# Ten of thirty convolution taps moved from VectorE to ScalarE and accumulating transfers

## The chip, the core and the metric

The kernel runs on one core of one Trainium2 chip. The metric is the device time of one execution in microseconds (us). Before the change the median of three runs is 1334.81 us.

The engines are called by the profile's names. PE is the matrix engine (TensorE), PEld its weight loads, DVE is VectorE, ACT is ScalarE, POOL is GpSimd and SP is SyncE. POOL and SP issue transfers (DMAs). Each engine works through its own instructions in a fixed order; an instruction whose inputs are not there holds up everything behind it on that engine.

## What is computed

One decoder layer over 1024 tokens of width 1024, in float32. Eleven 1024-wide projections of the normalised input feed three branches: a gated spatial mixing (A), a convolution module (B) and a cross-attention into 256 memory tokens (C). Each branch is projected, gated and summed, and an output projection and a norm follow. The change is in branch B:

```python
glu = z[..., OFF_B_A:OFF_B_A + W] * jax.nn.sigmoid(z[..., OFF_B_B:OFF_B_B + W])
c = causal_depthwise_conv(glu, conv_w[l], conv_b[l])     # 31 taps: position t sees t-30..t
c = jax.nn.silu(layer_norm(c, conv_ln_g[l], conv_ln_b[l]))
```

## The kernel before

**Tiles.** Features lie on the 128 partitions and tokens along the row, so a tile of 128 features by 1024 tokens is 512 KB. There are eight such tiles of the convolution, called conv tile 0 to 7 here. `slot()` hands out 36 buffers of that size (`NSLOT`) for everything that lives long: projection results, operands, branch values.

**Stages, in order of time.** Keys and values of the memory (to about 72 us); the first projection of branch A (to about 149 us); the other ten projections (149 to 928 us); the branch projections with the attention between them (928 to 1249 us); the output projection (to the end).

**The ten projections.** The loop at L546 goes over p = 0 to 3 and, inside, over ten blocks. Each call of `pair` (L373) makes two tiles of one block by seven products instead of eight (Strassen's scheme), each product being 12 matmuls of 128x512. float32 precision comes from splitting every operand into a high and a low part: ACT casts the high part (`split`, L74) and DVE subtracts it from the source to get the low part (L75). There are six operand buffers (`NOP`, tag `op`), so the two engines run a few products ahead of PE. Of a product's result in PSUM, ACT copies pieces (`p1` L383, `u2` L397, `u3` L404) and DVE adds others (L391, L405, L414); then ACT applies the block's function to the two result tiles `ca` and `cb` (L421 to L427), and POOL stores them. The matmuls of product `x<-T` for `os3` (L402) go on accumulating in the bank that the copy `u2` (L397) reads, so they wait for that copy. ACT's L421, the function of the previous pair's `ca`, stands just ahead of L397, and reads what DVE's L414 writes.

**The convolution.** `conv` (L449) is a generator: each of its steps is one DVE instruction. The first sets the accumulator `a` to the newest tap times the input plus the bias (L452), then thirty instructions (L456) each add one more tap, shifted by one token; then `a` is stored and added into `csum`. The generators of two tiles are queued in `todo` after block 1 of each p, and `pump` (L437) takes a few steps after each pair and eight after each branch tile (L727).

**The handover at about 928 us.** Merge 0 (`merge(0, 0)`, L725) projects branch A: 48 matmuls over eight feature tiles `bhi`/`blo` in order (L622). Each `bhi`/`blo` pair comes from `branch_tile` (L586): a cast on ACT, a subtraction on DVE. Behind them on DVE stand the low parts of the first attention queries (`ql`), which the score matmuls (L660) read.

**What sets the order.** A scheduler places all instructions of an engine in one list ahead of time. What the change does to these lists is shown below as rows of the built programs.

Of the kernel before, what the change touches and what calls it, by code (L numbers as in the profile page):

```python
# [10 lines left out]
AF = mybir.ActivationFunctionType  # L11
ALU = mybir.AluOpType
# [6 lines left out]
S = 1024  # L19
# [7 lines left out]
TAPS = 31  # L27
PAD = TAPS - 1
# [6 lines left out]
COL_CW = 56  # L35
# [4 lines left out]
def trunk(ctx, tc, xt, x, memt, wf, wv, wkf, wkv, wbr, wo, wst, bs, cols, fng, out):  # L40
    nc = tc.nc
    V, A, G, T = nc.vector, nc.scalar, nc.gpsimd, nc.tensor

    const = ctx.enter_context(tc.tile_pool(name="const", bufs=1))
    wpool = ctx.enter_context(tc.tile_pool(name="wpool", bufs=2))
    slots = ctx.enter_context(tc.tile_pool(name="slots", bufs=NSLOT))
    small = ctx.enter_context(tc.tile_pool(name="small", bufs=2))
# [10 lines left out]
    def slot(dt=F32, shape=(P, 1024), s="s"):  # L58
        return slots.tile(list(shape), dt, tag="slot", name=nm(s))
# [72 lines left out]
    def store(dst, src):  # L132
        G.dma_start(out=dst, in_=src)
# [6 lines left out]
    def spill(s, dt=F32, shape=(P, S)):  # L140
        return dram.tile(list(shape), dt, name=nm(s))

# [1 line left out]
    ones = const.tile([P, P], F32, name="ones")  # L144
    G.memset(ones, 1.0)
    onesd = const.tile([P, P], F32, name="onesd")
# [3 lines left out]
    col = const.tile([P, NCOL], F32, name="col")  # L150
    A.dma_start(out=col, in_=cols)

    def c1(base, k):
        return col[:, base + k:base + k + 1]

# [1 line left out]
    ahead = []  # L157

    def kv_ahead(n):
# [84 lines left out]
        if e >= XLAG:  # L244
            x_gain(e - XLAG)

# [1 line left out]
    B = [[[None] * 4 for _ in range(2)] for _ in range(2)]  # L248

    def x_norm(k, c):  # L250
# [15 lines left out]
    for hf in range(2):  # L266
        pst = [bank() for _ in range(MT)]
        for c in range(4):
            kv_ahead(KT + hf * 4 + c + NAHEAD)
            hi, lo = wchunk(None, ahead[KT + hf * 4 + c])  # L270
            i = hf * 4 + c
            if i < XLAG:
                x_gain(KT - XLAG + i)
            for m in range(MT):
                ms = slice(m * P, (m + 1) * P)
                for kk2 in range(2):
                    k = 2 * c + kk2
# [25 lines left out]
            split(o, q[:, 0, :], q[:, 1, :])  # L303
            lst.append(q)

# [1 line left out]
    nx = 0  # L307
    vadram = spill("vad", shape=(TT, P, D))
    for th in range(2):
        va = [slot(s="va") for _ in range(4)]  # L310
        for ch in range(2):
            pst = [bank() for _ in range(4)]
            for c in range(4):
                hi, lo = wchunk(None, raw_load(wv[ch * 4 + c], True))
                for t in range(4):
                    ts_ = slice(t * P, (t + 1) * P)
                    for kk2 in range(2):
                        k = 2 * c + kk2
# [5 lines left out]
                i = ch * 4 + c  # L324
# [15 lines left out]
            for t in range(4):  # L340
                A.activation(out=va[t][:, ch * H:(ch + 1) * H], in_=pst[t], func=AF.Gelu_apprx_tanh,
                             scale=1.0 if th else xrs[:, t:t + 1])
# [12 lines left out]
            A.activation(out=va[t], in_=va[t], func=AF.Identity, scale=vr[:, t:t + 1], bias=vm[:, t:t + 1])  # L355
            store(vadram[th * 4 + t], va[t])

# [1 line left out]
    pend = []  # L359

    def prod(ps, w, m, start, stop):
# [70 lines left out]
            then(ca, cb)  # L432
        return go

    todo = []

    def pump(n):  # L437
        while n and todo:
            try:
                next(todo[0])  # L440
                n -= 1
            except StopIteration:
                todo.pop(0)

    cdram = [spill("cd") for _ in range(KT)]

# [2 lines left out]
    def conv(e, g):  # L449
        cw = COL_CW + e * TAPS  # L450
        a = slot(s="conv") if e else csum
        V.tensor_scalar(a, g, col[:, cw + PAD:cw + PAD + 1], c1(COL_CB, e), ALU.mult, ALU.add)  # L452
        yield
        for j in range(PAD):
            n = S - PAD + j
            V.scalar_tensor_tensor(out=a[:, PAD - j:], in0=g[:, :n], scalar=col[:, cw + j:cw + j + 1],  # L456
                                   in1=a[:, PAD - j:], op0=ALU.mult, op1=ALU.add)
            yield
        store(cdram[e], a)
        if e:  # L460
            V.tensor_tensor(csum, csum, a, ALU.add)
            yield
# [16 lines left out]
    def hold(key):  # L479
        def then(ca, cb):  # L480
            held[key] = (ca, cb)
        return then

    def glu(p):
        def then(ca, cb):
            for i, (c, sg) in enumerate(zip((ca, cb), held.pop("b"))):
                V.tensor_tensor(c, c, sg, ALU.mult)
                todo.append(conv(2 * p + i, c))
        return then

    gate = {}
# [27 lines left out]
    def va_load(g):  # L519
        va = slot(shape=(P, TT, P), s="va")  # L520
        nc.sync.dma_start(out=va, in_=vadram[:, :, g * P:(g + 1) * P].rearrange("t p d -> p t d"))
        return va
# [23 lines left out]
    for p in range(4):  # L546
        for i, (blk, fn, then) in enumerate((
            (BLK_BB, sig, hold("b")),
            (BLK_BA, finish, glu(p)),
            (BLK_U, gelu, hold_u(p)),  # L550
            (BLK_GA, silu, ugate(p)),
            (BLK_GC, silu, to_dram(sgcdram)(p)),
            (BLK_GB, silu, to_dram(sgbdram)(p)),
            (BLK_Q, finish, to_dram(qdram)(p)),
            (BLK_M0, sig, to_dram(gdram[0])(p)),
            (BLK_M0 + 2, sig, to_dram(gdram[2])(p)),
            (BLK_M0 + 1, sig, to_dram(gdram[1])(p)),
        )):
            if p == 3 and i == 9:
                for e in range(NPRE):  # L560
                    bra[e] = load(udram[e], s="bra")
            if i == 2:
                spatial_load(p)
            pair(blk, p, kept(fn, then))
            if i == 3:
                for g in range(2 * p, 2 * p + NVA):
                    vas[g] = va_load(g)
            pump(PUMP[i])

# [1 line left out]
    ready = {}  # L571
    order = [(n, d) for n in (0, 2, 1) for d in range(KT)]
    raws = []
# [55 lines left out]
        V.tensor_tensor(g, ps, g, ALU.mult)  # L629
        return g  # L630

    # attention, half of the tokens of a head at a time, in four stages
    unit = {}
    brcdram = spills("brc")

# [121 lines left out]
    for d in range(KT):  # L757
        g = merge(2, d, conv_rstd if d == 4 else None)
# [44 lines left out]
    for d in range(KT):  # L803
        g = load(gdram[1][d], s="gate")
        ps = proj(1, d, bhi, blo)
        w = S if d < KT - 1 else H
        for i in range(0, S, w):
            v = slice(i, i + w)
# [5 lines left out]
        if d == W2AT:  # L814
            w21 = wbase(2)

# [1 line left out]
    def gop(v):  # L818
        o = op()
        split(v, o[:, 0, :], o[:, 1, :])  # L820
# [110 lines left out]
NPRE = 3  # L931
NRDY = 2
NFETCH = 3
NSLOT = 36
NRAW = 3
NOP = 6
NSUM = 4
# [58 lines left out]
```

## Time and profile before

| | before |
|---|---|
| median of three runs | 1334.81 us (1333.74 to 1335.65) |
| span of the profiled execution | 1333.8 us |
| PE busy | 1316.5 us, 99% |
| DVE busy | 1079.5 us, 81% |
| ACT busy | 595.3 us, 45% |
| POOL busy | 61.3 us, 5% |
| transfers, mean over the span | 135 GB/s |

The profile is one execution; its span runs from the first to the last instruction. The median of the timed runs is 1.0 us above that span. A share of busy time is an average over stages with different limits; what a change in one stage is worth is read from that stage's waits. The granted clock of PE is full in all of the 40 slices of the page.

### The profile page before, as it was taken

How to read it: one execution, taken by the hardware profiler on the slowest of the kernel's cores; microseconds unless marked ns; L12 is line 12 of the kernel's file. 1: busy time of each engine (PE TensorE's matmuls, PEld its weight loads, DVE VectorE, ACT ScalarE, POOL GpSimd, SP SyncE). 2: the span in 40 equal slices, each digit the busy share in tenths (PEclk: the TensorE clock that was granted, in tenths of full speed). 3: DMA queues.
4: the chain of work that ended last, by engine and by line, in shares of the span. 5: the costliest groups of instructions: out<-in, count | busy, mean ns of one | idle time of the engine just before them, and what ended most of it. 6: DMA issues, size and time to landing. Idle time of an engine off the chain costs nothing.

```text
span 1333.8 us, 16115 instructions
## 1 busy us (share of the span) xinstructions
PE 1316.5 (99%) x6084; PEld 1098.6 (82%) x6084; DVE 1079.5 (81%) x1438; ACT 595.3 (45%) x967; POOL 61.3 (5%) x120
## 2 busy tenths in 40 slices
PE   8999999999999999999999999999999999999997
PEld 7888888888888888888888888887888888888886
DVE  6799759969966998986996996796797486944797
ACT  6757634334444344434434444345544443502256
POOL 0000000000000000000000000001000010000000
PEclk9999999999999999999999999999999999999999
DMA  9634312342222333223333213338555354633323
GB/s 372 248 110 158 135 62 81 111 142 96 103 78 79 121 118 140 88 79 111 111 110 120 95 48 127 127 111 297 188 181 171 112 190 157 228 119 111 142 96 126
DMA packets 60126, 179.99 MB, mean 135 GB/s; under 512 B 5904, under 2 KB 15248, under 8 KB 60048
## 3 DMA queue, kind: packets, MB, share of 16 engines
q1 hardware_dynamic: 44464, 122.96, 27.2%
q0 software_dynamic: 15296, 55.58, 10.9%
q8 instruction: 47, 0.77, 0.2%
q10 hardware_dynamic: 288, 0.42, 0.1%
q14 instruction: 31, 0.25, 0.1%
HBM read 131.75 MB, written 47.19 MB: 134 GB/s over the span
## 4 chain that ended last, share of the span: by engine, by line
PE 95%; DVE 2%; ACT 1%; issue 0%; DMA 0%; SPq 0%; DVEq 0%; ACTq 0%
PE x L365 33%; PE acc L622 19%; PE y L365 16%; PE z L365 8%; PE b L322 6%; PE acc L841 5%; PE b L231 2%; PE acc L660 2%; PE acc L696 2%; PE b L280 1%; PE sp L534 1%; DMA mraw<-in_memt 0%; DVE xsum L130 0%; PE acc L681 0%; ACT y L874 0%
## 5 line engine op out<-in xcount | busy, mean ns | idle before, releaser
L365 PE MATMUL x<-T,op 128*128 128x512 f32 x1440 | 347.5, 390 | 0.7 <-ACT u L404 0.7
L365 PEld LDWEIGHTS x<-T,op 128*128 128x128 f32 x1440 | 269.8, 188 | 57.4 <-ACT u L404 1.1
L74 ACT CAST op<-sum 128x512 fp32r<-128x512 f32 x160 | 99.5, 622 | 132.2 <-PE z L365 56.4
L456 DVE SCALAR_TENSOR_TENSOR conv<-cb,col,conv 128x994 f32<-128x994 f32 (+14 forms) x120 | 151.8, 1265 | 0.5
L75 DVE TENSOR_TENSOR op<-sum,op 128x512 fp32r<-128x512 f32 x160 | 109.4, 686 | 36.0 <-ACT op L74 35.7
L622 PE MATMUL acc<-bhi,whi 128*128 128x512 f32 x384 | 119.7, 393 | 0.9 <-DVE ca L414 0.9
L622 PE MATMUL acc<-bhi,wlo 128*128 128x512 f32 x384 | 119.1, 390 | 0.0
L622 PE MATMUL acc<-blo,whi 128*128 128x512 f32 x384 | 118.7, 390 | 0.0
L365 PE MATMUL x<-B,op 128*128 128x512 f32 x480 | 115.5, 389 | 0.0
L365 PE MATMUL z<-B,op 128*128 128x512 f32 x480 | 115.3, 389 | 0.0
L365 PE MATMUL y<-T,op 128*128 128x512 f32 x480 | 115.3, 389 | 0.0
L365 PE MATMUL y<-B,op 128*128 128x512 f32 x480 | 115.3, 389 | 0.0
L456 DVE SCALAR_TENSOR_TENSOR conv<-ca,col,conv 128x994 f32<-128x994 f32 (+14 forms) x90 | 113.7, 1263 | 0.2
L74 ACT CAST op<-raw 128x512 fp32r<-128x512 f32 x120 | 74.3, 620 | 79.3 <-PE y L365 77.9
L75 DVE TENSOR_TENSOR op<-raw,op 128x512 fp32r<-128x512 f32 x120 | 82.1, 686 | 33.4 <-ACT op L74 33.4
L365 PEld LDWEIGHTS y<-B,op 128*128 128x128 f32 x480 | 90.1, 188 | 18.7
L365 PEld LDWEIGHTS y<-T,op 128*128 128x128 f32 x480 | 90.1, 188 | 18.7
L365 PEld LDWEIGHTS z<-B,op 128*128 128x128 f32 x480 | 90.1, 188 | 18.7
L365 PEld LDWEIGHTS x<-B,op 128*128 128x128 f32 x480 | 90.1, 188 | 18.7
L622 PEld LDWEIGHTS acc<-blo,whi 128*128 128x128 f32 x384 | 72.1, 188 | 15.5 <-DVE blo L75 0.4
L622 PEld LDWEIGHTS acc<-bhi,wlo 128*128 128x128 f32 x384 | 72.1, 188 | 15.0
L622 PEld LDWEIGHTS acc<-bhi,whi 128*128 128x128 f32 x384 | 71.3, 188 | 15.9 <-issue 1.7
(231 smaller groups left out, 1961.2 us busy)
## 6 DMA issues: line engine op xcount, KB each, us to landing
raw<-in_wf SPq DMA_DIRECT2D x80, 512.0 KB, 3.5
raw<-in_wbr SPq DMA_DIRECT2D x24, 512.0 KB, 4.4
gate<-g SPq DMA_DIRECT2D x24, 512.0 KB, 4.2
raw<-in_wv SPq DMA_DIRECT2D x16, 512.0 KB, 3.6
g<-cb POOLq DMA_DIRECT2D x12, 512.0 KB, 3.1
g<-ca POOLq DMA_DIRECT2D x12, 512.0 KB, 2.9
xr<-in_xt SPq DMA_DIRECT2D x8, 512.0 KB, 10.5
kvraw<-in_wkv SPq DMA_DIRECT2D x8, 512.0 KB, 10.7
```

The source lines that it names most:

```text
L74: A.copy(hi, src)
L75: V.tensor_tensor(lo, src, f(hi), ALU.subtract)
L231: T.matmul(ps[:, :M], w[:, ks], m[k], start=(k == 0 and j == 0), stop=(k == KT - 1 and j == 2))
L280: T.matmul(pst[m], a[k][:, ms], w[:, ws], start=(k == 0 and j == 0), stop=(k == KT - 1 and j == 2))
L322: T.matmul(pst[t], q[:, a, ts_], w[:, ws], start=(k == 0 and j == 0), stop=(k == KT - 1 and j == 2))
L365: T.matmul(ps, w[:, a, ks], m[k][:, b, :], start=(start and k == 0 and j == 0), stop=(stop and k == 3 and j == 2), skip_group_check=not start)
L456: V.scalar_tensor_tensor(out=a[:, PAD - j:], in0=g[:, :n], scalar=col[:, cw + j:cw + j + 1], in1=a[:, PAD - j:], op0=ALU.mult, op1=ALU.add)
L534: T.matmul(ps[:, t * P:(t + 1) * P], va[:, 4 * hf + t, :], ws[:, i, :], start=True, stop=True)
L622: T.matmul(ps[:, hf, :], w[:, ks], m[k][:, hf * H:(hf + 1) * H], start=(k == 0 and j == 0), stop=(k == KT - 1 and j == 2))
L660: T.matmul(ps[:, i, :], q[a][:, d, i * P:(i + 1) * P], kk[:, b, d, :], start=(d == 0 and j == 0), stop=(d == 1 and j == 2))
L696: T.matmul(ps[:, d, :], vv[:, a, m, d * P:(d + 1) * P], p2[b][:, m, :], start=(m == 0 and j == 0), stop=(m == MT - 1 and j == 2))
L841: T.matmul(ps[t], a[k][i][:, ts_], w[k][n], start=(start and k == 0 and j == 0), stop=(k == 3 and j == 2), skip_group_check=not start)
```

## The change

`conv` no longer runs wholly on DVE. ACT sets the accumulator (Identity with scale and bias). For the ten oldest taps ACT writes a scaled copy of the input into a new tile `tap`, and POOL issues a transfer that adds this tile into the accumulator in SBUF, shifted (`accum_op`). The other twenty taps stay on DVE, in a second generator `conv_rest` that is queued when the first is through. The first part has a queue of its own, `early`, of which three steps are taken after each pair, ahead of `pump`; what is left of it is taken after the loop. There are three more slots, and the scratch for transfer descriptors is set to 4096.

```diff
+    todo, early = [], []
+    def run(queue, n):
+        while n and queue:
+            try:
+                next(queue[0])
+                n -= 1
+            except StopIteration:
+                queue.pop(0)
+    def pump(n):
+        run(todo, n)
...
     def conv(e, g):
         cw = COL_CW + e * TAPS
         a = slot(s="conv") if e else csum
-        V.tensor_scalar(a, g, col[:, cw + PAD:cw + PAD + 1], c1(COL_CB, e), ALU.mult, ALU.add)
+        A.activation(out=a, in_=g, func=AF.Identity, scale=col[:, cw + PAD:cw + PAD + 1], bias=c1(COL_CB, e))
         yield
-        for j in range(PAD):
+        for j in range(NACT):
+            n = S - PAD + j
+            t = slot(s="tap")
+            A.activation(out=t[:, :n], in_=g[:, :n], func=AF.Copy, scale=col[:, cw + j:cw + j + 1])
+            G.dma_start(out=a[:, PAD - j:], in_=t[:, :n], accum_op=ALU.add)
+            yield
+        todo.append(conv_rest(e, g, a))
+
+    def conv_rest(e, g, a):
+        cw = COL_CW + e * TAPS
+        for j in range(NACT, PAD):
             n = S - PAD + j
             V.scalar_tensor_tensor(out=a[:, PAD - j:], in0=g[:, :n], scalar=col[:, cw + j:cw + j + 1],
                                    in1=a[:, PAD - j:], op0=ALU.mult, op1=ALU.add)
...
                 V.tensor_tensor(c, c, sg, ALU.mult)
-                todo.append(conv(2 * p + i, c))
+                early.append(conv(2 * p + i, c))
...
+            run(early, 3)
             pump(PUMP[i])
+    run(early, 10 ** 6)
...
-NSLOT = 36
+NACT = 10
+NSLOT = 39
...
+    nc = bacc.Bacc("TRN2", target_bir_lowering=False, num_devices=1, dynamic_dma_scratch_size=4096)
```

**Place 1: DVE at the handover.** The row of line, operation, what is written and read, and the size. Before, from the third `blo` of branch A to the gate of merge 0:

```order
L75 TENSOR_TENSOR blo_7362<-bra_7184,bhi_7361 128x1024
L414 TENSOR_TENSOR ca_7244<-y_7285,u_1227_7280 128x512
L75 TENSOR_TENSOR blo_7402<-bra_7399,bhi_7401 128x1024
L75 TENSOR_TENSOR blo_7408<-bra_7405,bhi_7407 128x1024
L75 TENSOR_TENSOR blo_7414<-bra_7411,bhi_7413 128x1024
L75 TENSOR_TENSOR blo_7420<-bra_7417,bhi_7419 128x1024
L75 TENSOR_TENSOR blo_7426<-bra_7423,bhi_7425 128x1024
L75 TENSOR_TENSOR ql_7430<-qf_7431,qh_7429 128x512
L75 TENSOR_TENSOR ql_7430<-qf_7435,qh_7429 128x512
L629 TENSOR_TENSOR gate_7439<-acc_7445,gate_7439 128x1024
```

The conv tile 7 comes only after these rows. With the change (`conv_6905` is conv tile 7; the first row is the second `blo`):

```order
L75 TENSOR_TENSOR blo_7543<-bra_7364,bhi_7542 128x1024
L469 SCALAR_TENSOR_TENSOR conv_6905<-cb_6206,col,conv_6905 128x1004
L75 TENSOR_TENSOR blo_7547<-bra_7366,bhi_7546 128x1024
L469 SCALAR_TENSOR_TENSOR conv_6905<-cb_6206,col,conv_6905 128x1005
L414 TENSOR_TENSOR ca_7426<-y_7467,u_1307_7462 128x512
L469 SCALAR_TENSOR_TENSOR conv_6905<-cb_6206,col,conv_6905 128x1006
L469 SCALAR_TENSOR_TENSOR conv_6905<-cb_6206,col,conv_6905 128x1007
L469 SCALAR_TENSOR_TENSOR conv_6905<-cb_6206,col,conv_6905 128x1008
L75 TENSOR_TENSOR blo_7587<-bra_7584,bhi_7586 128x1024
L469 SCALAR_TENSOR_TENSOR conv_6905<-cb_6206,col,conv_6905 128x1009
L469 SCALAR_TENSOR_TENSOR conv_6905<-cb_6206,col,conv_6905 128x1010
L469 SCALAR_TENSOR_TENSOR conv_6905<-cb_6206,col,conv_6905 128x1011
```

It goes on with three taps and one `blo` by turns, to the eighth `blo`:

```order
L75 TENSOR_TENSOR blo_7605<-bra_7602,bhi_7604 128x1024
L469 SCALAR_TENSOR_TENSOR conv_6905<-cb_6206,col,conv_6905 128x1018
L469 SCALAR_TENSOR_TENSOR conv_6905<-cb_6206,col,conv_6905 128x1019
L469 SCALAR_TENSOR_TENSOR conv_6905<-cb_6206,col,conv_6905 128x1020
L75 TENSOR_TENSOR blo_7611<-bra_7608,bhi_7610 128x1024
L75 TENSOR_TENSOR ql_7615<-qf_7616,qh_7614 128x512
L75 TENSOR_TENSOR ql_7615<-qf_7620,qh_7614 128x512
L469 SCALAR_TENSOR_TENSOR conv_6905<-cb_6206,col,conv_6905 128x1021
```

So seventeen taps of conv tile 7 (from 128x1004 to 128x1020) moved ahead of the eighth `blo`, which had none ahead of it. PE's order there is the same in both programs.

**Place 2: DVE and ACT where a tile's DVE taps begin** (p = 1, conv tile 2). DVE before:

```order
L391 TENSOR_TENSOR ca_3903<-z_3859,p_714_3872 128x512
L75 TENSOR_TENSOR op_3957<-sum_3851,op_3957 128x512
L75 TENSOR_TENSOR op_3975<-raw_3847,op_3975 128x512
L75 TENSOR_TENSOR op_3978<-sum_3852,op_3978 128x512
L456 SCALAR_TENSOR_TENSOR conv_3525<-ca_3157,col,conv_3525 128x1010
L414 TENSOR_TENSOR ca_3759<-y_3800,u_698_3795 128x512
```

DVE with the change (`conv_3418` is conv tile 2):

```order
L391 TENSOR_TENSOR ca_3967<-z_3923,p_745_3936 128x512
L75 TENSOR_TENSOR op_4042<-sum_3916,op_4042 128x512
L469 SCALAR_TENSOR_TENSOR conv_3418<-ca_3199,col,conv_3418 128x1004
L388 TENSOR_TENSOR sum_4067<-raw_4060,sum_4065 128x512
L469 SCALAR_TENSOR_TENSOR conv_3418<-ca_3199,col,conv_3418 128x1005
L414 TENSOR_TENSOR ca_3815<-y_3856,u_726_3851 128x512
```

ACT with the change (the tap copies stand where, before, the cast of the row ahead was followed by L423):

```order
L74 CAST op_4005<-sum_3913 128x512
L460 ACTIVATE tap_3893<-ca_3199,col 128x1002
L460 ACTIVATE tap_3896<-ca_3199,col 128x1003
L455 ACTIVATE conv_3899<-cb_3200,col 128x1024
L383 COPY p_745_3936<-x_3922 128x512
L423 ACTIVATE cb_3816<-cb_3816 128x512
L74 CAST op_4021<-sum_3915 128x512
L422 ACTIVATE cb_3816<-x_3770 128x512
L74 CAST op_4039<-raw_3911 128x512
L74 CAST op_4042<-sum_3916 128x512
L74 CAST op_4070<-raw_4060 128x512
L421 ACTIVATE ca_3815<-ca_3815 128x1024
```

The first DVE tap now stands two DVE taps ahead of L414, and reads what the last transfer of the tile adds. ACT's L397 follows the last row shown.

**Place 3: POOL's transfers** in the same stretch, with the change (before, only the rows of L133 stood there):

```order
L133 DMA sgc_1522<-cb_3641 128x1024
L461 DMA conv_3418<-tap_3754 128x1001
L133 DMA sgc_1521<-ca_3640 128x1024
L461 DMA conv_3418<-tap_3893 128x1002
L461 DMA conv_3418<-tap_3896 128x1003
L133 DMA sgb_1530<-cb_3816 128x1024
```

Each transfer of L461 waits until the one before it on the same tile has landed.

## Rows read from the trace of the kernel before

**Rows 1.** The page, part 1: busy us (share of span) xinstructions

```profile
PE 1316.5 (99%) x6084; PEld 1098.6 (82%) x6084; DVE 1079.5 (81%) x1438; ACT 595.3 (45%) x967; POOL 61.3 (5%) x120
```

**Rows 2.** PE's waits: engine, line, releaser, total us, times, longest

```profile
PE b L231 <- ACT mhi L187: 6.2, 2, 5.9
PE acc L622 <- DVE ca L414: 0.9, 1, 0.9
PE x L365 <- ACT u L404: 0.7, 1, 0.7
PE acc L121 <- DVE dg L120: 0.6, 1, 0.6
PE b L322 <- DVE wlo L75: 0.4, 1, 0.4
```

**Rows 3.** Groups by line, x count: ns min/median/max; ACT group with busy us, mean ns

```profile
L456 DVE SCALAR_TENSOR_TENSOR conv<-ca,col,conv x90: 1245/1265/1283, 429.6 to 908.5; 128x994 f32<-128x994 f32 x3, 128x995 f32<-128x995 f32 x3, 128x996 f32<-128x996 f32 x3, 128x997 f32<-128x997 f32 x3
...
L452 DVE TENSOR_SCALAR conv<-cb,col x4: 807/807/807, 301.5 to 949.6; 128x1024 f32<-128x1024 f32 x4
...
L421 ACT ACTIVATE ca<-ca 128x1024 f32<-128x1024 f32 x32 | 34.0, 1062 | 11.7 <-DVE ca L414 10.1
```

**Rows 4.** POOL's transfers: KB and us to landing; its queue: packets, MB, share

```profile
cd<-conv POOLq DMA_DIRECT2D x7, 512.0 KB, 3.3
...
g<-ca POOLq DMA_DIRECT2D x12, 512.0 KB, 2.9
...
v<-vd POOLq DMA_DIRECT2D x4, 512.0 KB, 8.3
...
q0 software_dynamic: 15296, 55.58, 10.9%
```

**Rows 5.** Timeline, ACT, 457 to 471 us: start, duration, what, [idle before]

```profile
457.12 0.62 ACT L74 CAST op<-sum 128x512 fp32r<-128x512 f32 x1
...
469.16 1.06 ACT L421 ACTIVATE ca<-ca 128x1024 f32<-128x1024 f32 x1 [1.02 <-DVE ca L414]
470.24 0.59 ACT L397 COPY u<-x 128x512 f32<-128x512 f32 x1
```

**Rows 6.** Timeline, DVE, 453 to 469 us, and 907 to 910 us

```profile
453.54 1.26 DVE L456 SCALAR_TENSOR_TENSOR conv<-ca,col,conv 128x1004 f32<-128x1004 f32 x1
454.72 0.69 DVE L75 TENSOR_TENSOR op<-raw,op 128x512 fp32r<-128x512 f32 x1
455.32 1.26 DVE L456 SCALAR_TENSOR_TENSOR conv<-ca,col,conv 128x1005 f32<-128x1005 f32 x1
...
468.44 0.68 DVE L414 TENSOR_TENSOR ca<-y,u 128x512 f32<-128x512 f32 x1
...
907.14 2.60 DVE L456 SCALAR_TENSOR_TENSOR conv<-ca,col,conv 128x1022 f32<-128x1022 f32 x2
909.66 0.68 DVE L75 TENSOR_TENSOR op<-raw,op 128x512 fp32r<-128x512 f32 x1
```

**Rows 7.** Timeline, PE, 470 to 476 us

```profile
470.04 2.88 PE L365 MATMUL y<-T,op 128*128 128x512 f32 x12
472.76 2.88 PE L365 MATMUL x<-T,op 128*128 128x512 f32 x12
```

**Rows 8.** Timeline at the handover: ACT, DVE and PE, 921 to 940 us

```profile
921.71 0.59 ACT L404 COPY u<-x 128x512 f32<-128x512 f32 x1 [1.62 <-PE x L365]
922.20 1.05 ACT L74 CAST bhi<-bra 128x1024 fp32r<-128x1024 f32 x1
...
925.24 1.23 DVE L75 TENSOR_TENSOR blo<-bra,bhi 128x1024 fp32r<-128x1024 f32 x1 [0.51 <-ACT bhi L74]
...
930.88 5.77 DVE L75 TENSOR_TENSOR blo<-bra,bhi 128x1024 fp32r<-128x1024 f32 x5 [2.06 <-ACT bhi L74]
...
928.97 0.70 PE L622 MATMUL acc<-bhi,whi 128*128 128x512 f32 x2 [0.88 <-DVE ca L414]
...
939.62 0.85 PE L622 MATMUL acc<-blo,whi 128*128 128x512 f32 x3
```

**Rows 9.** Timeline, PE, the first matmuls of the program

```profile
8.46 0.41 PE L231 MATMUL b<-mlo,whi 128*128 128x256 f32 x1
...
15.66 0.28 PE L231 MATMUL b<-mhi,whi 128*128 128x256 f32 x1
```

More of the change, by code (lines that the diff above doesn't have):

```diff
@@ L433, in kept @@
         return go
-    todo = []
-    def pump(n):
-        while n and todo:
+    todo, early = [], []
+    def run(queue, n):
+        while n and queue:
             try:
-                next(todo[0])
+                next(queue[0])
                 n -= 1
             except StopIteration:
-                todo.pop(0)
+                queue.pop(0)
+    def pump(n):
+        run(todo, n)
     cdram = [spill("cd") for _ in range(KT)]
@@ L988 @@
     arrays = {k: np.ascontiguousarray(v) for k, v in arrays.items()}
-    nc = bacc.Bacc("TRN2", target_bir_lowering=False, num_devices=1)
+    nc = bacc.Bacc("TRN2", target_bir_lowering=False, num_devices=1, dynamic_dma_scratch_size=4096)
     args = [nc.dram_tensor(k, v.shape, mybir.dt.from_np(v.dtype), kind="ExternalInput").ap() for k, v in arrays.items()]
```

## The prediction

> **What bounds the kernel now.** I read the busy time first: PE works 1316.5 of the 1333.8 us of the profiled execution [rows 1]. At most 17.3 us are idle. PE's waits say what that is: one of 6.2 us at the head, where the first operand has yet to come, and then four of 0.9, 0.7, 0.6 and 0.4 us, each once [rows 2]; the rest, some 8.5 us, is the tail after the last matmul. So the waits that a less busy DVE could take away are 0.9 + 0.7 + 0.6 + 0.4 = 2.6 us in all. DVE is busy for 81% and ACT for 45%, and neither holds PE. What the change can gain is 2.6 us at most; what it can lose has no such limit, because PE has no slack: whatever a matmul needs and gets later is lost. So the question is which of PE's operands come later.
>
> **The change part by part.**
>
> *Work that changes engine.* DVE loses 8 tiles x 10 taps x 1.265 us and 8 inits x 0.807 us [rows 3]: 101.2 + 6.5 = 107.7 us. ACT gains 88 passes over a row of about 1024. The nearest row is its L421, 1.06 us [rows 3]: 93 us, which takes ACT from 595 to about 689 us, 52%. Both lie beside PE's products, so by themselves they change nothing: 0 us. If the cover is gone, a tap copy costs the 1.06 us by which it delays the next cast; that is counted below where it happens.
>
> *The accumulating transfer.* The trace has no transfer that adds into its destination, so its price L must be bounded. POOL's plain stores of the same 512 KB land 2.9 to 3.3 us after the issue, and its slowest 512 KB transfers take 8.3 us [rows 4]. An addition must read the destination as well as the source. POOL's queue moved 55.58 MB in 10.9% of 16 engines' 1333.8 us [rows 4]: 0.109 x 1333.8 = 145.4 us of all 16 engines, or 1.37 us for 524 KB. I add one such pass to the store out of `conv`: L = 3.3 + 1.3 = 4.6 us, between 2.9 and 8.3. It is nearer to the store, since both start in SBUF, while the 8.3 us row is a load of another layout. Transfers on one tile run in series, since each waits for the one before.
>
> The Trainium skill speaks against a cheap add: in "Collectives: The Full Stack" (section "The bandwidth ceiling: the fold count and why AG ≠ RS ≠ AR") an add inside a transfer needs two source reads on one read ring and so runs at half the copy's rate. "DMA: Bandwidth & Descriptors" of the Trainium skill (section "Anatomy of one DMA — SWDGE (gpsimd) path") fits a transfer by 2.0 us plus its bytes by 436 KB per us, an estimate of 3.2 us for 512 KB, with which the 3.3 us of the trace agrees. With two reads that estimate is 4.4 us, and the sum below would be some 2 us lower; no run here shows it yet.
>
> *The handover, the main term.* Before, DVE had no tap of conv tile 7 ahead of branch A's eighth `blo`; with the change there are seventeen (place 1). DVE works in order, so these taps and the `blo` rows between them run as one row. When does it begin? The last tap copy of tile 7 stands on ACT right behind the copy `u` at 921.71 us, where before the first `bhi` cast began at 922.20 us [rows 8]. So it runs from 922.2 to 923.3, its transfer lands at 923.3 + 4.6 = 927.9, and the first DVE tap, which reads what it added to, starts then. DVE waits for it with the remaining `blo` rows queued behind. A tap on DVE takes from 1.18 us (453.54 to 454.72) to 1.30 us (two in 2.60) [rows 6]; I take 1.25. A `blo` takes 5.77 / 5 = 1.15 us [rows 8], and L414 takes 0.60 us, the pitch of a 512-wide row [rows 6]. From the first tap to the end of the eighth `blo` stand 17 taps, 6 `blo` rows and one L414: 21.25 + 6.9 + 0.6 = 28.75 us, so to 956.65 us. Before, PE took the eighth `blo` at 939.62 us without waiting [rows 8]. PE's order there is unchanged, so PE loses 956.65 - 939.62 = 17.0 us. The attention rows behind, `ql` first, follow at DVE's old pitch and cost no more.
>
> This term hardly hangs on L. With L = 2.9 the first tap waits for the second `blo` instead, which stood at 925.24 us for 1.23 us [rows 8], so it starts no earlier than about 926.4 and the loss is 15.5 us; with L = 6.3 it is 18.7 us, with 8.3 20.7 us. With all taps at 1.18 us it is 1.2 us less.
>
> *Where a tile's DVE taps begin.* For the even tiles the last two tap copies stand on ACT behind the cast at 457.12 us [rows 5] (place 2): they end at 457.12 + 0.62 + 1.06 = 458.8 and at 459.9. The two transfers run in series and land at 463.4 and 468.0 us. DVE's first tap of the tile cannot start before 468.0; behind it stand a sum (0.60), a second tap and L414, which then runs 470.96 to 471.64. Before, it started at 468.44 [rows 6]. ACT's L421 waits for L414 and takes 1.08 us (469.16 to 470.24), the copy `u` behind it 0.59 us [rows 5]: done at 473.3 us. PE's `x<-T`, which waits for that copy, started at 472.76 us [rows 7]. So PE loses 0.55 us there, at four even tiles 2.2 us. Here L counts twice: at 4.3 us the loss is gone, at 6.3 us it is 4.0 us each. Odd tiles have a single transfer in their last group; I take 0 for them, and the even tile's loss as the bound.
>
> *The rest.* Stores on POOL now stand behind accumulating transfers that wait for their tiles. Where a store is late, only its slot comes free later, and three slots are added: 0 us, the cover being those slots. If POOL's 8.3 us loads [rows 4] were held behind waiting transfers, it would cost one or two of them, up to 16 us; I see no such place near PE's operands and keep it for the range. The smaller descriptor scratch: 0, with the same bound.
>
> **Sum.** 1333.8 + 17.0 + 2.2 = 1353.0 us for a profiled execution. The median stood 1.0 us above the span of the profile before; with that, 1354, and rounded for what waits I left at 0, **1355 us**.
>
> **The rivals.**
>
> *(a) The freed DVE time shows.* DVE drops to about 973 us, PE's 2.6 us of small waits go, and nothing else is late: 1334.8 - 2.6 = 1332 us, or no change. It would need the eighth `blo` by 939.62 us. From 927.9 us that leaves 11.7 us, of which 7.5 go to `blo` and L414, so seventeen taps in 4.2 us, 0.25 us each against 1.25 measured. It could be only if PE had other work there. Its order is unchanged, and the next matmuls are those of the same merge. Chance 0.06: 0.02 for faster, 0.04 for no change.
>
> *(b) Slow transfers.* One pair takes 7 x 2.72 us (470.04 to 472.76 [rows 7]) = 19.0 us, and three steps are taken per pair. From L = 6.3 us on, three transfers in series don't fit into a pair, the chain falls behind, and L414 and with it PE wait at every tile. At 6.3 us: 1334.8 + 18.7 + 8 x 4.0 = 1385.5 us. At 8.3 us the 20 transfers of a p take 166 us where seven pairs last 133, so some 33 us per p are left over: 1334.8 + 20.7 + 4 x 33 = 1487 us. For it: nothing in the trace shows an addition in a transfer. Against it: L would have to be double the store. Chance 0.17.
>
> *(c) PE's clock falls at the handover.* From 928 to 957 us PE would have some 10 us of work in 28 us. Before, the granted clock is full in every slice, but at the program's start, after PE had stood idle, a matmul of 128x256 took 0.41 us at 8.46 us and 0.28 us at 15.66 us [rows 9]. If the lower level comes back and lasts as long as from the one row to the other, 7.2 us at half the speed, 3.6 us of work are lost: 1355 + 3.6 = about 1359 us. For it: the gaps. Against it: PE gets eight short groups of matmuls in that stretch and is never idle for its whole length. Chance 0.12.
>
> "TensorE: Matmul & The Clock Gate" of the Trainium skill (section "HAM oscillation — how this bites in real kernels") says that gaps in TensorE's work make the clock fall again, which is the case (c). No row before the change shows it after the head.
>
> **How the numbers follow.** The forecast, handover plus small losses, has 0.65: 1348 to 1362 us. Its low end is L = 2.9 with no loss at the even tiles and the shortest taps: 1334.8 + 15.5 - 1.2 = 1349, less part of the 2.6 us. The range reaches down to 1346, where all of these 2.6 us are won back as well (1349.1 - 2.6 = 1346.5), and up to 1390, which takes in (c), the 6.3 us case of (b) and a late load; above it lies the worse half of (b), below it lies (a). A measurement of this kernel can tell about 0.2% (2.7 us) from no change; slower by more than that are the forecast, (b) and (c): 0.94. No change 0.04, faster 0.02.
>
> **What would show it.** In the profile after: a wait of PE at the merge's line (L638 now) for DVE, about 17 us in all between 929 and 957 us, DVE without a gap there and taps of the last `conv` tile between its `blo` rows; in the chain, a share for DVE's conv line in that stretch alone; issues `conv<-tap` that land 4 to 5 us after; waits of PE for the copy `u` of half a us at even tiles; ACT at about 690 us and DVE at about 973 us busy. The granted clock in the slices around 930 to 965 us decides on (c). I am wrong if the transfers take over 6 us, if PE waits in the ten projections at every tile, or if the wait at the merge is well under 15 us, which would mean that the taps didn't stand in DVE's way.

## The result, and the profile after

The changed kernel takes 1389.51 us (median of 4 runs, 1385.57 to 1393.42) against 1335.23 before: 4.1% slower, ratio 1.0409, interval 1.0388 to 1.0431. Forecast were 1355 us, so the sign was right and the size was not: 54 us lost in place of 20. The profiled execution spans 1386.7 us, 52.9 more than the one before.

The page of the profile after, the busy line [rows 1 before], the granted clock by slices, the transfers that POOL issues (queue q0, before in [rows 4]), and the medians from issue to landing for the new transfers, by size:

```profile
PE 1331.5 (96%) x6084; PEld 1105.3 (80%) x6084; DVE 984.7 (71%) x1350; ACT 677.5 (49%) x1055; POOL 130.0 (9%) x200
...
PEclk9999999999999999999999999998799999999999
...
q0 software_dynamic: 26816, 96.49, 26.9%
...
conv<-tap POOLq DMA_DIRECT2D x7, 501.5 KB, 6.1
conv<-tap POOLq DMA_DIRECT2D x7, 501.0 KB, 5.6
conv<-tap POOLq DMA_DIRECT2D x7, 500.5 KB, 6.9
...
conv<-tap POOLq DMA_DIRECT2D x7, 497.0 KB, 4.5
```

DVE and ACT moved as meant: DVE 94.8 us less, ACT 82.2 more. PE does the same 6084 matmuls and is busy for 15.0 us longer; the windows below show that its clock was lower in places. PE's waits after, as engine, line, releaser, total us, times, longest [rows 2 before]:

```profile
PE x L365 <- ACT u L397: 20.5, 7, 4.8
PE acc L638 <- DVE ca L414: 11.3, 1, 11.3
PE acc L638 <- DVE blo L75: 7.1, 4, 2.8
```

So there are two places. **The tiles**: seven waits for the copy `u` in the ten projections, one for each conv tile but the last. **The handover**: 18.4 us at the merge. Two lines of PE's timeline divide the loss. The last product of the projections, `y<-B`, starts at 953.90 us, where before it started at 925.21: 28.7 us are lost up to there. The score matmuls of `ql` follow 39.77 us later (993.67), where before it was 15.56 us (925.21 to 940.77): 24.2 us more. Together 52.9 us, the whole difference. The two lines of before:

```profile
925.21 2.88 PE L365 MATMUL y<-B,op 128*128 128x512 f32 x12
...
940.77 0.28 PE L660 MATMUL acc<-k,ql 128*128 128x256 f32 x1
```

PE at the tiles (start, duration, what, idle before and who ended it): the first tile, the second and the third, and last the handover's end and start of the stretch above.

```profile
280.20 5.49 PE L365 MATMUL x<-T,op 128*128 128x512 f32 x12 [3.96 <-ACT u L397]
...
360.93 3.02 PE L365 MATMUL x<-T,op 128*128 128x512 f32 x12 [1.68 <-ACT u L397]
...
482.72 4.61 PE L365 MATMUL x<-T,op 128*128 128x512 f32 x12 [3.19 <-ACT u L397]
...
953.90 2.88 PE L365 MATMUL y<-B,op 128*128 128x512 f32 x12
968.05 1.19 PE L638 MATMUL acc<-bhi,whi 128*128 128x512 f32 x2 [11.27 <-DVE ca L414]
...
993.67 0.28 PE L676 MATMUL acc<-k,ql 128*128 128x256 f32 x1
```

The same twelve matmuls take 2.88 us elsewhere. After the four waits of 3.19 to 4.82 us (even tiles) they take 4.38 to 5.49 us, after the three of 1.46 to 1.68 us (odd tiles) 3.01 to 3.04. The windows of 8 us behind the waits show it as clock (columns: window, length, busy us of PE, PEld, DVE, ACT and POOL, granted clock, DMA share, GB/s):

```profile
280.00:288.00 8.00, 7.80 (x23) 6.23 (x24) 6.75 (x8) 3.46 (x7) 0.53 (x1) 0.64 0.38 131
482.00:490.00 8.00, 7.28 (x25) 5.84 (x26) 7.64 (x10) 4.34 (x8) 0.76 (x2) 0.79 0.40 131
```

Summed over the group of the `x<-T` matmuls, busy us and mean ns, before (first) and after (second):

```profile
L365 PE MATMUL x<-T,op 128*128 128x512 f32 x1440 | 347.5, 390 | 0.7 <-ACT u L404 0.7
```
```profile
L365 PE MATMUL x<-T,op 128*128 128x512 f32 x1440 | 356.3, 397 | 21.2 <-ACT u L397 20.5 <-ACT u L404 0.7
```

So the tiles cost 20.5 us of waiting (15.7 at the four even tiles, 4.8 at the three odd ones) and 8.8 us of slower matmuls behind it: 29.3 us, of which 28.7 reach the end.

**One tile, step by step** (conv tile 2, the place of rows 5 to 7). First POOL's issues, then DVE, then ACT:

```profile
465.67 0.83 POOL L461 DMA_DIRECT2D conv<-tap  x1 [5.39 <-ACT tap L460]
471.30 0.84 POOL L461 DMA_DIRECT2D conv<-tap  x1 [4.79 <-issue]
```
```profile
477.45 1.26 DVE L469 SCALAR_TENSOR_TENSOR conv<-ca,col,conv 128x1004 f32<-128x1004 f32 x1 [4.65 <-DMA conv<-tap]
478.64 0.68 DVE L388 TENSOR_TENSOR sum<-raw,sum 128x512 f32<-128x512 f32 x1
479.24 1.26 DVE L469 SCALAR_TENSOR_TENSOR conv<-ca,col,conv 128x1005 f32<-128x1005 f32 x1
480.42 0.68 DVE L414 TENSOR_TENSOR ca<-y,u 128x512 f32<-128x512 f32 x1
```
```profile
481.13 1.06 ACT L421 ACTIVATE ca<-ca 128x1024 f32<-128x1024 f32 x1 [6.39 <-DVE ca L414]
482.10 0.57 ACT L397 COPY u<-x 128x512 f32<-128x512 f32 x1
```

From the first issue to the second are 5.6 us (the first landed 5.1 us after its issue), from the second to DVE's tap 6.15 us. DVE stands idle for 4.65 us with L414 behind the tap; ACT's L421 waits for L414, the copy `u` stands behind L421, and PE waits for the copy. This is the chain of the prediction, row by row; only the transfers are longer. At the four even tiles the first of the two landed after 4.4 to 5.1 us and the second after 6.1 to 8.1, and from the first issue to DVE's tap 11.8 to 13.2 us passed.

**The handover.** DVE's timeline there, [rows 8] before:

```profile
954.46 1.23 DVE L75 TENSOR_TENSOR blo<-bra,bhi 128x1024 fp32r<-128x1024 f32 x1 [0.24 <-ACT bhi L74]
963.73 1.26 DVE L469 SCALAR_TENSOR_TENSOR conv<-cb,col,conv 128x1004 f32<-128x1004 f32 x1 [8.04 <-DMA conv<-tap]
...
991.37 1.22 DVE L75 TENSOR_TENSOR blo<-bra,bhi 128x1024 fp32r<-128x1024 f32 x1
```

The row of seventeen taps, six `blo` and one L414 runs from 963.73 to 992.59 us, 28.9 us; 28.75 were worked out. But it begins 9.8 us after the start of `y<-B`, where 2.7 us were forecast (927.9 against 925.21 us). POOL's issues tell why: the last transfer was not alone.

```profile
933.80 0.85 POOL L461 DMA_DIRECT2D conv<-tap  x1 [7.61 <-ACT tap L460]
943.43 0.87 POOL L461 DMA_DIRECT2D conv<-tap  x1 [8.78 <-ACT whi L74]
...
951.26 0.83 POOL L461 DMA_DIRECT2D conv<-tap  x1 [6.39 <-DMA conv<-tap]
...
957.38 0.87 POOL L461 DMA_DIRECT2D conv<-tap  x1 [4.75 <-issue]
```

The last tap copy was there at 952.0 us (950.89 us plus 1.14), but the transfer before it was itself held until 951.26; the last one went out 6.1 us behind it, and DVE's tap began 6.35 us after that. The three transfers of the group ahead had landed 9.05, 7.24 and 5.61 us after their issues, each issued some 0.5 us behind the landing before it: 23.1 us (933.80 to 956.87) where a pair lasts 19.0, so the chain of transfers had fallen behind. While the first two moved, SP's queue moved 1.98 and 1.45 MB.

### The profile page after: what moved, and what is told of

It reads as the page before. It is cut to its first block, busy times and chain, and to the rows that moved or that the text cites. A ratio compares the mean times of both kernels' runs of the same rounds, so it can differ in the third digit from the quotient of the medians.

```text
span 1386.7 us, 16307 instructions
## 1 busy us (share of the span) xinstructions
PE 1331.5 (96%) x6084; PEld 1105.3 (80%) x6084; DVE 984.7 (71%) x1350; ACT 677.5 (49%) x1055; POOL 130.0 (9%) x200
## 3 DMA queue, kind: packets, MB, share of 16 engines
q1 hardware_dynamic: 44464, 122.96, 26.3%
## 5 line engine op out<-in xcount | busy, mean ns | idle before, releaser
L365 PE MATMUL x<-T,op 128*128 128x512 f32 x1440 | 356.3, 397 | 21.2 <-ACT u L397 20.5
L365 PEld LDWEIGHTS x<-T,op 128*128 128x128 f32 x1440 | 274.5, 191 | 82.3 <-ACT u L397 23.9
L638 PE MATMUL acc<-bhi,whi 128*128 128x512 f32 x384 | 122.6, 400 | 11.3 <-DVE ca L414 11.3
L469 DVE SCALAR_TENSOR_TENSOR conv<-cb,col,conv 128x1004 f32<-128x1004 f32 (+9 forms) x80 | 101.4, 1267 | 15.2 <-DMA conv<-tap 14.7
L365 PEld LDWEIGHTS y<-T,op 128*128 128x128 f32 x480 | 90.1, 188 | 18.7
L365 PEld LDWEIGHTS z<-B,op 128*128 128x128 f32 x480 | 90.1, 188 | 18.7
L365 PEld LDWEIGHTS y<-B,op 128*128 128x128 f32 x480 | 90.1, 188 | 18.7
L461 POOL DMA_DIRECT2D conv<-tap x70 | 59.7, 852 | 391.7 <-ACT tap L460 196.9
L74 ACT CAST whi<-raw 128x1024 fp32r<-128x1024 f32 x40 | 41.9, 1053 | 96.9 <-PE acc L638 69.9
## 6 DMA issues: line engine op xcount, KB each, us to landing
kvraw<-in_wkv SPq DMA_DIRECT2D x8, 512.0 KB, 11.8
```

The source lines that it names most:

```text
L74: A.copy(hi, src)
L365: T.matmul(ps, w[:, a, ks], m[k][:, b, :], start=(start and k == 0 and j == 0), stop=(stop and k == 3 and j == 2), skip_group_check=not start)
L461: G.dma_start(out=a[:, PAD - j:], in_=t[:, :n], accum_op=ALU.add)
L638: T.matmul(ps[:, hf, :], w[:, ks], m[k][:, hf * H:(hf + 1) * H], start=(k == 0 and j == 0), stop=(k == KT - 1 and j == 2))
```

## The experiments

**Theory A**: DVE's place in the order times the landing of the transfers. DVE works in order, so a tap that waits for a transfer holds up L414 at the tiles and the `blo` rows at the handover. **Rival B**: the transfers load the DMA queues so much that loads and stores on the path are late, wherever the taps stand. In a second step, what makes a landing 4.4 or 7 us long.

### Only the order, at the handover

`held7` takes the place of `conv_rest` for the last conv tile; `gates` holds the gate rows of DVE, and the first tap is put behind the first of them in DVE's order:

```diff
-        todo.append(conv_rest(e, g, a))
+        todo.append(held7(e, g, a) if e == KT - 1 else conv_rest(e, g, a))
+
+    def held7(e, g, a):
+        while not gates:
+            yield
+        rest = conv_rest(e, g, a)
+        with tc.issue_after(gates[0].ins):
+            next(rest)
+        yield
+        yield from rest
...
-        V.tensor_tensor(g, ps, g, ALU.mult)
+        gates.append(V.tensor_tensor(g, ps, g, ALU.mult))
```

> One edit to the changed kernel: the twenty DVE taps of the last conv tile stand behind the gate of merge 0 on DVE, as they did before the change. Theory A (the loss is DVE working in order behind transfers that land late: 24.2 us at the handover, from the start of y<-B to the score matmuls of ql 39.8 us against 15.6 before, and 28.9 us at the seven other conv tiles, stalls and slow clock together): the handover comes back whole, 1389.5 - 24 = about 1365 us, and PE waits less than 2 us at the merge. Rival B (the transfers hurt through the DMA queues: stores, weights and branch values arrive later wherever they stand): the merge keeps a wait for another operand and less than half of the 24 us comes back, over 1377 us.

Measured: 1367.71 us (1363.16 to 1368.52). From `y<-B` to `ql` it is 17.08 us in place of 39.77. PE waits at the merge for 0.9 us on `ca` as before and 0.6 us more. So 22 of the handover's 24 us come back with the transfers untouched: theory A at the handover. The seven waits at the tiles stay (22.3 us).

### Only the order, at the tiles

The lists in `late` are handed to `todo` HOLD = 2 pairs later, and `keep` holds the first tap in program order on DVE:

```diff
-        todo.append(conv_rest(e, g, a))
+        late[HOLD - 1].append(conv_rest(e, g, a))
...
+            if j == NACT:
+                keep(ins)
```

> One edit to the changed kernel: the DVE taps of every conv tile are queued two pairs later, the first of them held in program order on DVE, so that the tile's last transfer has some 19 us more to land. Theory A: the waits of PE for the copy u at seven tiles go, and the slow clock behind four of them: 28.9 us, to about 1360 us; the handover keeps its 24 us. Rival B (the DMA queues are overfull, so that the chain of transfers falls behind whatever stands on DVE): the stalls move with the taps and over 1375 us are left.

> Both edits, the last conv tile's taps behind the gate and the other tiles' two pairs later. Theory A: both losses go and nothing is left of the change but DVE's relief: 1333 to 1338 us, the time of the kernel before, within 0.3% of it. Rival B: over 1345 us. Rival C (the freed DVE time is worth something once the waits are gone): under 1332 us.

Measured: 1368.1 us with this edit alone, 1349.86 us with both (ratio 1.011, 1.0095 to 1.0125). The waits for the copy `u` are gone in both, but each came 8 to 12 us short of what was expected, and by the mark set beforehand (over 1345 us) the run with both falls to rival B. With both edits PE's waits name new causes:

```profile
PE x L365 <- DVE op L75: 6.7, 3, 2.6
...
PE acc L653 <- ACT bhi L74: 2.8, 1, 2.8
```

At the first of the three, DVE's addition into a new `ca` (L391) had stood 1.37 us for `DMA conv<-tap`: most likely there was no slot until a transfer had landed that still read its `tap`. At the merge, ACT's cast had waited 6.34 us for a branch value to load. Holding a tile two pairs longer costs slots. That is a loss by the edit and not rival B, if a shorter hold is free of it; the next run decides.

### The order, with a short hold

The same, but the first DVE tap of a tile directly behind the L414 that it held up (one pair later in the queue, and `tc.issue_after` on that L414), the last tile behind the gate.

> As in the run with both edits, but the first DVE tap of the tiles 0 to 6 stands directly behind the L414 that it held up, and not two pairs later; the last tile's taps stay behind the gate. Theory A (nothing but the order on DVE costs, and what the two-pair version still lost, 14 us, came from tiles that kept their slots longer: a new ca that waited for a tap's slot, a branch value that loaded late): those losses go too, 1334 to 1341 us. Rival B (the transfers' traffic itself holds up loads and stores on the path): a remainder of 8 us or more stays, 1343 us or more.

Measured: 1338.28 us (1337.77 to 1339.82), ratio 1.0031, 1.0019 to 1.0043. The same eighty transfers, the same engines, the same busy times (ACT 679.4, DVE 985.1 us); PE's busy time is back at 1316.5 us. Of 54 us, 51 were order. PE's waits there:

```profile
PE x L365 <- ACT u L397: 1.8, 2, 1.1
...
PE acc L655 <- DVE ca L414: 0.9, 1, 0.9
```

The transfer still lands late at conv tile 2, and DVE still stands for it; but L414 is ahead of it now, and the wait costs nothing:

```profile
466.81 0.69 DVE L414 TENSOR_TENSOR ca<-y,u 128x512 f32<-128x512 f32 x1 [0.60 <-PE y L365]
470.16 1.26 DVE L483 SCALAR_TENSOR_TENSOR conv<-ca,col,conv 128x1004 f32<-128x1004 f32 x1 [2.65 <-DMA conv<-tap]
```

### Only the price: transfers that don't add

The eighty transfers without `accum_op=ALU.add`, in the changed kernel's order.

> The changed kernel with the additions left out of the eighty transfers: each writes its 512 KB without reading the destination, so the convolution is wrong by the ten taps. The order on all engines is the same. Theory A with the price of a transfer made of a fixed part and the bytes read: issue to landing falls from 4.9 us median (4.4 at best) to about 3.2; the even tiles' stalls go (at 4.3 us they were worked out to be gone), the odd ones too, and the handover is left with DVE's row of 28.8 us behind the second low part: 15 to 18 us lost, 1350 to 1353 us. Rival D (it is the place of the taps on DVE, not the price of the addition, that costs at the tiles): the stalls stay, 1375 us or more.

Measured: 1354.65 us. Landing 2.8 us at best and 2.9 median (4.4 and 4.9 with the addition). No wait at the tiles is left, and the handover takes 33.22 us, 17.7 more than before. The total is 1.7 us above the range expected for this run. That it is also the forecast's 1355 us is chance: for L = 2.9 the prediction gives 15.5 us at the handover, and here it was 17.7, because here too the last transfer was held by the one before it, which took 7.09 us (918.60 to 925.69), so that DVE's row began 3.3 us after `y<-B` in place of 1.2:

```profile
929.58 1.26 DVE L469 SCALAR_TENSOR_TENSOR conv<-cb,col,conv 128x1004 f32<-128x1004 f32 x1 [1.49 <-DMA conv<-tap]
```

Queue q0:

```profile
q0 software_dynamic: 21696, 96.49, 18.5%
```

The bytes counted are the same, the time is not. The share times the span is what all 16 engines spent: 145.4 us before, 250.2 here, 373.0 with the addition. If the queue's other transfers took what they took before, a plain 500 KB transfer cost (250.2 - 145.4) / 80 = 1.31 us of all engines and an adding one (373.0 - 145.4) / 80 = 2.85, 2.2 times as much. The best landings differ by about the same, 4.4 - 2.8 = 1.6 us.

That an add takes two source reads and so runs at about half the copy's rate is the rule in the Trainium skill's "Collectives: The Full Stack" (section "The bandwidth ceiling: the fold count and why AG ≠ RS ≠ AR"), there for transfers between cores; the 2.2 times agree with it. The estimate from the Trainium skill's "DMA: Bandwidth & Descriptors" (section "Anatomy of one DMA — SWDGE (gpsimd) path"), 4.4 us with two reads, is what the best landings here took; its estimate for a plain transfer of this size, 3.2 us, is above the 2.8 measured.

### Half the size

Every adding transfer cut to 512 columns (256 KB).

> The changed kernel with every adding transfer cut to 512 of some 1000 columns (256 KB), so that half of the ten taps' part is missing. The order is the same. If the price is a fixed part and one part for each byte read and written, then by the plain transfers' 2.8 us and the adding ones' 4.4 us at best the second read of 512 KB costs 1.6 us; half the bytes then land in about 2.8 to 3.1 us, as the plain ones of full size, and the time is that of the run with plain transfers, 1352 to 1357 us. If the addition has a fixed price per transfer, the landing stays at 4 us or more and the time above 1365 us.

Measured: 1366.36 us, 9 us over the expected range. The landing is 3.3 us median, 3.2 at best, a little above the expected; a fixed price per addition is out by the landing, though the time alone would have fallen to that case (above 1365 us). At the tiles 3.1 us of waits for `u` and 2.8 for operands are left. Most of the rest is at the handover, 37.5 us from `y<-B` to `ql`: there the last transfer, though half as long, landed 8.6 us after its issue, while SP's queue moved 2.38 MB. It was issued at 932.49 us, and DVE's tap began at 941.64:

```profile
941.64 1.27 DVE L469 SCALAR_TENSOR_TENSOR conv<-cb,col,conv 128x1004 f32<-128x1004 f32 x1 [5.78 <-DMA conv<-tap]
```

The median of a transfer says little about the one that counts.

### What makes a landing longer

The landings of 6 to 7 us stand beside others of 4.5 with nearly the same bytes. Two suspects share the time of a tile's last transfers: stores behind them on POOL's own queue, and weight loads on SP's.

> The changed kernel without the sixteen stores of the sgc and sgb tiles, which are issued right behind the last transfers of the even tiles (the loads of them read other tiles in their place, so branches B and C are wrong). Theory E (a transfer that adds takes 4.4 us alone and some 1.4 us more for every other 512 KB that moves at the same time): the last two transfers of the even tiles land 4.5 to 5 us after the issue in place of 5.9 and 6.1, the wait for the copy u at the four even tiles falls from 3.2 to 4.8 us each to about 1 us, the slow clock behind it goes as well, and the handover stays: 1368 to 1376 us. Rival F (the longer landings have another cause, as the length of the series or the issue): landings and stalls stay, 1385 us or more.

Measured: 1393.14 us, no better. The waits for `u` are 22.1 us, and the last two transfers of the even tiles land as late as before (median of the four tiles 4.5 and 7.2 us, with the stores 4.4 and 7.1). The stores were not it. For the loads more traffic was put on SP's queue, two copies from memory to memory per pair, which nothing waits for:

```diff
+        for j in range(2):
+            keep(nc.sync.dma_start(out=spill("extra"), in_=wf[blk, 2 * p + j]))
```

> The changed kernel with two more 512 KB copies from memory to memory per pair, issued behind the pair's two weight loads on SP's queue; nothing waits for them. Theory E2 (a transfer that adds takes 4.4 us alone and longer when a load of another queue moves at the same time; stores behind it on POOL's own queue don't matter, as the run without stores showed): where such a copy falls together with a tile's last two transfers, they land 1 to 2 us later each, the waits for the copy u at the seven tiles grow from 20.5 to 30 us or more, and with the slow clock the time goes to 1400 us or more. Rival F (the landing has its spread from the length of the series on POOL): waits and time as before, 1386 to 1394 us.

> The control: the same eighty copies in the kernel before the change. Both theories: PE's operands are some products ahead, so 1334 to 1338 us, no wait of PE over 1 us that was not there.

Measured: 1427.68 us, 38 us more than the changed kernel, as theory E2 had it in the time but not in the place: the last two transfers of the even tiles together landed no later (median 5.6 and 5.0 us, without the copies 4.4 and 7.1). Earlier ones of a tile took 8 to 10 us, and the series behind them came late. The same copies in the kernel before changed nothing (1333.89 against 1333.93 us, ratio 0.9999). Waits and two of the landings with the copies (6.9 and 4.5 us without):

```profile
PE x L365 <- ACT u L399: 50.7, 7, 9.1
PE acc L640 <- DVE ca L416: 11.9, 1, 11.9
```
```profile
conv<-tap POOLq DMA_DIRECT2D x7, 500.5 KB, 9.5
...
conv<-tap POOLq DMA_DIRECT2D x7, 499.0 KB, 8.8
```

So traffic on SP's queue lengthened landings, and the stores behind the transfers on their own queue didn't. The trace of the changed kernel has it too. Of its eighty transfers the 28 during which SP's queue began under 0.05 MB landed after 4.39 to 5.10 us; the 32 with 0.3 to 0.6 MB, about one weight load, after 6.1 us in the median (4.46 to 8.11). One of them: while the last transfer of tile 2 moved (471.3 to 477.4 us), SP's queue (q1: packets, MB, share) moved one weight load:

```profile
q1 hardware_dynamic: 144, 0.52, 30.5%
```

In the run without stores the same was so for two of three transfers of that tile, which took 6.2 and 5.9 us, and the one without a load took 5.0. The Trainium skill's "DMA: Bandwidth & Descriptors" (section "Queues, rings and completion order") says that an engine takes turns between the queues that have work, which fits both runs.

Before the change the weight loads had the same neighbours as now, less the eighty transfers, and PE's operands were ahead by some products. The control fits that: 42 MB more traffic (122.96 to 164.91 MB on SP's queue) cost nothing. It is the change that put a landing on the path.

### Fewer taps, and the small parts

> The changed kernel with five taps on ScalarE in place of ten. On DVE the last conv tile is then nearly through at the handover: one tap and the csum sum stand ahead of the fourth low part, none behind. Theory A (place, not number): the handover loses 4 us at most in place of 24, and the tiles lose by where their first DVE tap stands against the third of three transfers in series: 1338 to 1352 us. Rival G (the loss goes with the number of transfers): half of the loss, about 1362 us.

> Five taps on ScalarE, and the last conv tile's DVE taps behind the gate of merge 0. Theory A (order alone costs; DVE's relief brings nothing as PE has no waits to give back): the 3.3 us wait at the merge goes as well, 1334 to 1336.5 us, within 0.2% of the kernel before. If DVE's relief were worth something by itself: under 1332 us.

> The kernel before with only the change's three more slots and the smaller descriptor scratch. All theories: no effect, 1333 to 1337 us. If the smaller scratch held up POOL's transfers, over 1338 us.

Measured: five taps 1338.3 us (ratio 1.0031, 1.002 to 1.0042); with the last tile behind the gate as well 1335.11 us (1.0006, 0.9997 to 1.0015); slots and scratch alone 1334.49 us (1.0001, 0.9991 to 1.001). With half of the transfers not half of the loss is left but 3.8 us. PE's waits name no tile any more; they name 3.3 us for `ca` at the merge, which the second edit brings back to the 0.9 us of before. The last profile of five taps has the waits of the kernel before and one more of 0.2 us at the head, with DVE at 1026.3 us in place of 1079.5 and ACT at 640.3. VectorE is relieved there, and nothing is faster: PE had no wait to give back. No version beat the kernel before.

## Why the prediction missed

Of the 34 us between forecast and result, 27 are at the tiles (2.2 forecast, 29.3 lost) and 7 at the handover. Two of the prediction's own signs of being wrong came true: transfers over 6 us, and waits in the ten projections at nearly every tile.

**What bounds the kernel, and the upper limit of the gain**: right. With five taps and the last tile behind the gate PE has the waits of before again, and the time is that of before.

**The mechanism at both places**: right, to the row. DVE's row at the handover took 28.9 us (28.75 worked out), and PE lost the 17.0 us that follow from it and what its head came late; the tiles' chain went from the transfer over tap, L414, L421 and the copy `u` to PE.

**The price L, 4.6 us for every transfer: the term that failed.** It was built as a store plus one more read, and that is near what an undisturbed transfer costs: 4.4 us at best, 4.9 median over eighty. But the median was not the right number. The sum used one value for all, and the last transfer of an even tile, beside a weight load, landed after 6.1 to 8.1 us. Two in series to DVE's tap took 11.8 to 13.2 us in place of 2 x 4.6 = 9.2. The prediction's rule was right: 0.55 us plus what the two take longer is 3.1 to 4.6 us, and PE waited 3.2 to 4.8; at conv tile 2 it is 0.55 + 2.6 = 3.15, and 3.19 were measured. The case "4.0 us each at L = 6.3" stood among the rivals (slow transfers, 0.17), bound to the condition that the chain of transfers falls behind by the pair; at the tiles it needed no such thing, since two transfers in series at the end of a tile were enough. That this rival's 1385.5 us is near the result is luck: it had eight waits of 4.0 us and 18.7 us at the handover, and no clock.

**The handover, 17.0 us forecast, 24.2 lost.** The step that failed is "its transfer lands at 923.3 + 4.6". It took the last transfer alone, issued as soon as its copy was there. The chain had fallen behind at this tile, the condition that the prediction had put under slow transfers: the last one went out 5.35 us behind its copy, and from its issue to DVE's tap passed 6.35 us in place of 4.6. The head of DVE's row came 7.1 us later than forecast, and 17.0 + 7.1 = 24.1, against 24.2 measured. The text said that this term hardly hangs on L; it hangs on how long each of the transfers in series ahead of it takes.

**The clock, rival (c): right in kind, wrong in place.** At the handover the granted clock fell to 0.50, the lower of the two levels (columns as in the windows above):

```profile
980.00:985.00 5.00, 2.26 (x5) 1.82 (x6) 4.93 (x5) 0.00 (x0) 0.00 (x0) 0.50 0.00 0
```

But there PE waits for DVE (4.93 of 5 us busy), and a slower matmul only fills the wait. Row and head account for the 24.2 us without it; and where the tiles alone were held, the granted clock from `y<-B` to `ql` was lower, 0.65 in the mean of 40 us against 0.70, and the stretch as long, 39.88 us against 39.77. The clock cost at the tiles, 8.8 us, where PE has a full queue behind the wait; nothing was put down for that.

**The odd tiles, taken as 0:** 1.46 to 1.68 us each, above the 0.55 that was to be their bound. Their last transfer was not a slow one (4.5 us). At conv tile 3, at 548 us, POOL had stood 6.43 us in front of the mask of the spatial weights, waiting for their load, and the tile's last transfer was queued behind it, out at 548.73 us though its tap copy had ended at 546.6. DVE's four taps ahead of L414 did the rest. The prediction asked what is queued behind the new transfers on POOL, and not what they are queued behind.

**Parts at zero**: slots and scratch, right by themselves. DVE's relief was counted in durations, 107.7 us. The durations of DVE's instructions added up did fall by 108.6 us (1171.3 to 1062.7), but the busy time counts the overlap of two neighbours once and fell by 94.8.

**The range**: 1390 held the median by half a us, by luck and for the wrong case. Its chances rested on one price for all transfers; the spread between transfers was not in it.

## What to carry to other kernels

Work moved to a transfer has no fixed price: take the landing at the place where somebody waits for it, with the loads that move beside it, and count how many stand in series there. Ask of each waiting instruction what stands behind it on its engine: here the taps' place in DVE's order, behind L414 and behind the gate, was worth 51 of the 54 us with the transfers as slow as before. And relieving an engine that PE did not wait for brought nothing in any of these versions.

## What the runs showed of the hardware

- An accumulating transfer of 500 KB within SBUF took 4.4 us at best from issue to landing, a plain one 2.8; half the bytes with the addition 3.2. Of the DMA engines' time it took an estimated 2.85 us against 1.31, and POOL was busy 0.85 us with the issue against 0.55.
- Adding transfers landed after 4.39 to 5.10 us with next to nothing on SP's queue beside them, and after 6.1 us in the median beside about one weight load. Two more 512 KB copies per pair on SP's queue brought the fifth and the eighth of a tile's ten to 8.8 and 9.5 us median. Without the stores behind them on their own queue the last two of a tile landed no sooner.
- After waits of 3.2 to 4.8 us PE worked at the lower clock: twelve matmuls took 4.4 to 5.5 us in place of 2.88, so that a wait of 3.96 us cost 6.6 in all. The length of the wait alone does not settle it: 2.52 us were followed by 4.50 us in the run without stores, 2.31 us by 3.02 in the one with the last tile held. A kernel that keeps PE busy through such a wait was not tried.
